# Output projection of a decoder layer: three pairs of row blocks multiplied by seven products each

## The chip, the cores and the metric

The kernel runs on one core of one Trainium2 chip. A core has a matrix engine (PE), a vector engine (DVE), a scalar engine (ACT), GpSimd (POOL) and a queue engine (SP) that only issues transfers. The time is the device time of one execution in microseconds; the time of the kernel before is the median of three runs. A profile of one execution gives the start and end of every instruction, counted from the first one.

## The reference

One decoder layer, 512 positions of width 1024, in float32. The change touches the output projection `mix`: the 2048 columns `[h, y]` (four mLSTM heads of 256 columns, then 1024 columns of a convolution group) times `w_out`, 2048 x 1024.

```python
u = rms_norm(x, mix_pre_g[l]) * (1.0 + sc1) + sh1
proj = u @ w_in[l]
...
h = mlstm_chunkwise(heads(q), heads(k), heads(v), ...)
h = rms_norm(h, ml_norm_g[l].reshape(H, Dh)).reshape(Bsz, S, D_ML)
h = h * jax.nn.sigmoid(o_pre)
...
y = causal_dwconv(a * jax.nn.sigmoid(gt), cv_dw_w[l], cv_dw_b[l])
y = jax.nn.silu(layer_norm(y, cv_ln_g[l], cv_ln_b[l]))

mix = jnp.concatenate([h, y], axis=-1) @ w_out[l]
x = x + g1 * rms_norm(mix, mix_post_g[l])

u = rms_norm(x, ffn_pre_g[l]) * (1.0 + sc2) + sh2
up = causal_dwconv(u @ ffn_up[l], ffn_conv_w[l], ffn_conv_b[l])
...
x = x + g2 * rms_norm(f, ffn_post_g[l])
```

## The kernel before

**Products.** Matrices are kept as a high part (rounded to the fast float32 format of PE) and a low part (the rest). `mm3` (lines 207 to 210) makes one product of a 128-row block by three matmuls: high by high, high by low, low by high. A weight piece, 128 x 512, is split by `w_split` (line 191: ACT copies the high part; line 192: POOL or DVE subtracts for the low part). `w_load` (line 199) loads up to four pieces at once into one of two `raws` buffers through SP's queue and splits them; the split pieces live in 20 `wpool` tiles, two a piece. Most other 128 x 512 tiles come from 36 `slots`; four `cvs` tiles (`cvtile`) serve as scratch. PSUM has four banks "mm", two "at" and two "cv".

**Order.** PE's and SP's instructions run in program order. The order on DVE, ACT and POOL is made at build time by a scheduler that simulates the engines and takes the ready instruction of highest priority, in general the one earliest in the program; `tc.cur_priority += LATER` puts what follows behind everything else. Each engine then executes its list in order. `behind(...)` and the manual dependence in `ada_block` force one instruction to stand after another on an engine.

**Heads.** `head_load` and `head_proj` make queries and keys, `make_vo` the values and the output gate (`vo`, one token tile of 128 positions after the other, eight row blocks each), `attention` (line 543) the scores (`s`, line 551), the outputs (`o`, line 562), the normalisation (lines 574 to 587) and the transposes (`hT`, line 593); lines 599 and 600 then split each of a head's two blocks of 128 columns into `hh` and `hl`. `attention` and `make_vo` are generators; `next(steps)` and `next(values)` lay their parts between the projections. The convolution taps run meanwhile on DVE, ACT and POOL; `norm_mean`, `norm_sums`, `norm_rows` and `norm_tiles` (lines 814 to 841) normalise their result into the eight blocks `yh`, `yl`. 

**Projection.** The sixteen row blocks of `w_out` are taken in the order `MIX`: heads 0 to 2 (blocks 0 to 5), y 8 to 13, head 3 (6 and 7), y 14 and 15. The left half of the 1024 output columns goes first (`mix_first`, into the four banks `mixa`, one for a token tile), between the steps of head 3's attention. The right half follows in the banks `mixb`: the first eight blocks in the loop at line 943, the other eight in `mix_last`, tile by tile, where each finished tile goes into the chain of norms (`chain_sums`, `chain_x`, `chain_u`) and on to the feed-forward part.

**Conditioning sums.** `ada_block` (line 176) loads half a megabyte through ACT's queue and multiplies it with the condition on DVE, summing each row. Sums 16 to 23 give the gains of `mixa`; sums 24 to 39 stand behind `last_lo`, head 3's last `hl`. They use two `ada` buffers and four parts of `spare`, which lies in the place of `u`'s low half once the last values are made. `ada_done` (line 181) and lines 948 to 950 make the gains of the feed-forward norm, `send_rows` (line 692) transposes them on PE (`gT`), stores them in DRAM and `row` loads them back as rows (`gs2r`, `sh2r`).

## Time and profile before

| | us |
|---|---|
| runs of the kernel | 767.45, 768.76, 769.22 (median 768.76) |
| span of the profiled execution | 767.4 |
| PE busy | 756.0 |
| DVE busy | 576.6 |
| POOL busy | 516.5 |
| ACT busy | 410.7 |
| mixa on PE, 192 matmuls of 128 x 512 | 317.2 to 368.5, with other pieces between |
| mixb up to `gT`, 96 matmuls | 368.5 to 390.3 |

The profile gives the execution's span, from its first to its last instruction; its time with what lies around the span isn't listed apart. A row of the timeline has the start, the duration, the engine, the line of the kernel, the operation, out<-in with their shapes, and in brackets how long the engine was idle before it and what released it. A row of the chain has start, duration, engine, what. PE's order on the chain is the program's, so the chain from 314 to 403 us shows the whole projection.

### The profile page before, as it was taken

The numbers are of one execution on the slowest core, as the hardware profiler recorded it, in microseconds if no ns is written. First come the engines' busy times: TensorE is split into PE (matmuls) and PEld (weight loads), VectorE is DVE, ScalarE is ACT, GpSimd is POOL, SyncE is SP. The second block draws the span as 40 slices with busy tenths as digits, with TensorE's granted clock in tenths as the row PEclk, the third lists the DMA queues.
The fourth block names the chain that finished last, engine by engine and source line by source line (L and its number), as shares of the span: only waits on it lengthen the run. The fifth ranks groups of instructions, "written<-read, shape, count | busy, mean of one in ns | idle before, by whom it ended". The sixth has DMA issues, their size and how long they took to land.

```text
span 767.4 us, 10129 instructions
## 1 busy us (share of the span) xinstructions
PE 756.0 (99%) x3480; PEld 625.1 (81%) x3480; DVE 576.6 (75%) x837; ACT 410.7 (54%) x778; POOL 516.5 (67%) x428
## 2 busy tenths in 40 slices
PE   7999999999999999999999999999999999999996
PEld 5778898878788788888889988888888888888885
DVE  6669999979979696476989978675684775654547
ACT  6675428585665655573345444443534444566633
POOL 4779849796494872645631179786887884599943
PEclk9999999999999999999999999999999999999999
DMA  8973313411131241655965755666767565796273
GB/s 317 349 281 113 112 56 117 158 56 56 55 111 56 98 168 64 235 199 168 365 222 183 271 210 191 240 219 247 262 231 275 187 239 185 271 397 241 93 249 135
DMA packets 40136, 147.32 MB, mean 192 GB/s; under 512 B 3826, under 2 KB 5266, under 8 KB 30484
## 3 DMA queue, kind: packets, MB, share of 16 engines
q1 hardware_dynamic: 27524, 96.59, 34.9%
q10 hardware_dynamic: 12560, 50.08, 18.3%
q8 instruction: 27, 0.44, 0.2%
q14 instruction: 25, 0.20, 0.1%
HBM read 126.59 MB, written 20.07 MB: 191 GB/s over the span
## 4 chain that ended last, share of the span: by engine, by line
PE 93%; DMA 4%; POOL 1%; ACT 1%; issue 0%; DVEq 0%; SPq 0%; DVE 0%; POOLq 0%; ACTq 0%
PE up L210 31%; PE dn L210 13%; PE qko L210 13%; PE vo L210 9%; PE glu L210 7%; PE mixa L210 6%; PE mixb L210 6%; DMA wglu<-in_w_glu 3%; PE o L562 2%; PE s L551 2%; PE v L210 2%; PE glu L350 1%; DMA xn<-in_x 1%; PE xT L992 0%; PE hT L593 0%
## 5 line engine op out<-in xcount | busy, mean ns | idle before, releaser
L774 DVE SCALAR_TENSOR_TENSOR cv<-gt,cvw,cv 128x485 f32<-128x485 f32 (+24 forms) x200 | 137.2, 731 | 2.1 <-ACT cv L762 0.8
L770 POOL TENSOR_TENSOR cs<-cs,cs 128x510 f32<-128x510 f32 (+3 forms) x32 | 42.1, 1316 | 0.2
L192 POOL TENSOR_TENSOR wup_0l<-wup,wup_0h 128x512 fp32r<-128x512 f32 x18 | 25.0, 1389 | 19.4 <-ACT wup_0h L191 19.3
L210 PE MATMUL up<-u2h,wup_0h 128*128 128x512 f32 (+1 forms) x96 | 35.8, 373 | 0.0
L210 PE MATMUL up<-u2h,wup_0l 128*128 128x512 f32 (+1 forms) x96 | 35.7, 371 | 0.0
L210 PE MATMUL up<-u2h,wup_512h 128*128 128x512 f32 (+1 forms) x96 | 35.6, 371 | 0.0
L210 PE MATMUL up<-u2l,wup_512h 128*128 128x512 f32 (+1 forms) x96 | 35.6, 371 | 0.0
L210 PE MATMUL up<-u2h,wup_512l 128*128 128x512 f32 (+1 forms) x96 | 35.6, 371 | 0.0
L210 PE MATMUL up<-u2l,wup_0h 128*128 128x512 f32 (+1 forms) x96 | 35.6, 371 | 0.0
L210 PE MATMUL up<-u2h,wup_1024h 128*128 128x512 f32 (+1 forms) x92 | 35.0, 381 | 0.0
L210 PE MATMUL up<-u2l,wup_1024h 128*128 128x512 f32 (+1 forms) x92 | 34.9, 380 | 0.0
L210 PE MATMUL up<-u2h,wup_1536l 128*128 128x512 f32 (+1 forms) x92 | 34.9, 380 | 0.0
L210 PE MATMUL up<-u2h,wup_1536h 128*128 128x512 f32 (+1 forms) x92 | 34.9, 380 | 0.0
L210 PE MATMUL up<-u2l,wup_1536h 128*128 128x512 f32 (+1 forms) x92 | 34.9, 380 | 0.0
L210 PE MATMUL up<-u2h,wup_1024l 128*128 128x512 f32 (+1 forms) x92 | 34.9, 380 | 0.0
L176 DVE SCALAR_TENSOR_TENSOR junk<-ada,cb 128x1024 bf16<-128x1024 f32 x20 | 29.9, 1493 | 2.6 <-DMA ada<-in_adaT 2.5
L768 ACT ACTIVATE cs<-gt,cvw 128x511 f32<-128x511 f32 (+4 forms) x40 | 27.1, 713 | 6.1 <-POOL cs L770 3.5
L192 POOL TENSOR_TENSOR wup_1536l<-wup,wup_1536h 128x512 fp32r<-128x512 f32 x18 | 24.6, 1365 | 6.0 <-ACT wup_1536h L191 5.4
L191 ACT ACTIVATE wup_512h<-wup 128x512 fp32r<-128x512 f32 x22 | 13.8, 629 | 25.7 <-PE up L210 20.9
L192 POOL TENSOR_TENSOR wup_1024l<-wup,wup_1024h 128x512 fp32r<-128x512 f32 x18 | 23.6, 1314 | 5.0 <-ACT wup_1024h L191 5.0
L330 DVE SCALAR_TENSOR_TENSOR junk<-ada,cps 128x1024 bf16<-128x1024 f32 x16 | 19.5, 1220 | 9.8 <-DMA ada<-in_adaT 9.2
L1113 DVE TENSOR_TENSOR b<-b 128x512 f32<-128x512 f32 x11 | 19.4, 1762 | 8.6 <-POOL b L1112 8.6
(1097 smaller groups left out, 2726.8 us busy)
## 6 DMA issues: line engine op xcount, KB each, us to landing
wup<-in_w_up SPq DMA_DIRECT2D x22, 1024.0 KB, 5.0
b<-in_w_down ACTq DMA_DIRECT2D x11, 1024.0 KB, 5.1
spill_t<-b ACTq DMA_DIRECT2D x11, 1024.0 KB, 3.9
ada<-in_adaT ACTq DMA_DIRECT2D x20, 512.0 KB, 4.8
wqko<-in_w_qko SPq DMA_DIRECT2D x9, 1024.0 KB, 4.8
ada<-in_adaT SPq DMA_DIRECT2D x16, 512.0 KB, 7.5
wo<-in_w_out SPq DMA_DIRECT2D x8, 1024.0 KB, 5.5
wvo<-in_w_vo SPq DMA_DIRECT2D x6, 1024.0 KB, 4.8
```

The lines of the kernel that those rows point to most:

```text
L176: t = V.scalar_tensor_tensor(out=junk, in0=r, scalar=1.0, in1=cb, op0=ALU.mult, op1=ALU.mult, accum_out=mod[:, i : i + 1])
L191: S.activation(hi[:, :n], src, AF.Copy)
L192: (eng or G).tensor_tensor(out=lo[:, :n], in0=src, in1=hi[:, :n].bitcast(F32), op=ALU.subtract)
L210: PE.matmul(ps, l, r, start=start and i == 0, stop=stop and i == 2, skip_group_check=again)
L330: V.scalar_tensor_tensor(out=junk, in0=first[k][:, i * D : (i + 1) * D], scalar=1.0, in1=cps, op0=ALU.mult, op1=ALU.mult, accum_out=part[: ...
L350: PE.matmul(ps, blk(wk, i)[a], u[k][b], start=k == 0 and p == 0, stop=k == KT - 1 and p == 1)
L551: PE.matmul(sp[:, :n], ks[d][:, cc * P : (cc + 1) * P], qs[d][:, cc * P :], start=d == 0, stop=d == 1)
L562: PE.matmul(o[:, : DH + 2], E[h][cc][:, a : a + P], vs[h][cc], start=cc == 0, stop=cc == tt)
L768: S.activation(t[:, d:], cvx[j][:, : T - d], AF.Copy, scale=w(CK - 1 - d))
L770: G.tensor_tensor(out=side[:, d:], in0=side[:, d:], in1=t[:, d:], op=ALU.add)
L774: tap = V.scalar_tensor_tensor(out=cp[:, d:], in0=cvx[j][:, : T - d], scalar=w(CK - 1 - d), in1=cp[:, d:], op0=ALU.mult, op1=ALU.add)
L1113: V.tensor_tensor(out=b22, in0=b22, in1=b11, op=ALU.subtract)
```

## The change

Each of heads 0 to 2 gives a pair of row blocks. With the 512 tokens cut into two halves of 256 (`HT`), the pair's two blocks of columns are a 2 x 2 matrix of left blocks, and the two row blocks of `w_out` with two halves of 512 columns are a 2 x 2 matrix of right blocks. The change makes the 2 x 2 result by seven block products (Winograd's form) and not eight: "11", "12", "22", "s1", "s2", "s3", "s4". "11", "12" and "s4" use blocks of `w_out` as they are; "s2", "s3", "22" and "s1" use sums of blocks. The sums of weights `mixq[1]` to `mixq[4]` are made in DRAM, by four copies on SP's queue and four adding transfers on POOL's. `left_parts` makes high and low parts and the sums of left blocks on ACT and POOL; `sums_split` splits the sums later. In `mixa` five products are made; the partial results K1, U2 and U3 are copied out of the banks into `cvs` tiles (`kept`) in between, and come in again by DVE, U2 and U3 in `mixb`, where "s1" and "s4" follow. A pair's weight loads are three pieces (`right_load`), of which every third piece's low part is made on DVE. The ten other blocks (`PLAIN`) stay as they were; in `mixb` two of them (`EARLY`) are laid between "s1" and "s4", and eight are left for `mix_last` as before. The values of head 3's last two token tiles are made together, block by block. Sums 24 to 27 of `ada_block` stand behind the last `yl` and no longer behind `last_lo`.

```diff
-MIX = [*range(6), *range(8, 14), 6, 7, 14, 15]
+PLAIN = [*range(8, 14), 6, 7, 14, 15]
+NP = len(PLAIN)
+PAIRS = 3
...
+        for tt in range(NT if h < H - 1 else 2):
+            ps = mmbank(f"vo{h}_{tt}")
+            some(tt, ps, range(KT))
+            values_out(tt, ps)
+            yield
+        if h == H - 1:
+            both = [mmbank(f"vo{h}_{tt}") for tt in (2, 3)]
+            for k in range(KT):
+                for tt, ps in zip((2, 3), both):
+                    some(tt, ps, [k])
+                if k == KT // 2 - 1:
+                    yield
+            for tt, ps in zip((2, 3), both):
+                values_out(tt, ps)
             yield
...
+    def left_parts(h, e, y):
+        z = left[h]
+        if e == 0:
+            halfy[h] = y
+            a11 = slot(f"ma{h}", F32R)
+            S.activation(a11[:, :HT], y[:, :HT], AF.Copy)
+            minus(a11[:, HT:], y[:, :HT], a11[:, :HT].bitcast(F32))
+            z["11"] = a11[:, :HT], a11[:, HT:], 0
+            return
+        x = halfy.pop(h)
+        hi, lo = slot(f"mh{h}", F32R), slot(f"ml{h}", F32R)
+        S.activation(hi, y, AF.Copy)
+        minus(lo, y, hi.bitcast(F32))
+        z["12"], z["22"] = (hi, lo, 0), (hi, lo, HT)
+        z["14"], z["23"] = a, b = slot(f"ms14_{h}"), slot(f"ms23_{h}")
+        minus(a[:, :HT], x[:, HT:], y[:, HT:])
+        minus(b[:, :HT], a[:, :HT], x[:, :HT])
+        minus(b[:, HT:], x[:, :HT], x[:, HT:])
+        G.tensor_tensor(out=a[:, HT:], in0=y[:, :HT], in1=b[:, :HT], op=ALU.add)
...
+    def mix_copies():
+        for q, a in ((1, 0), (3, 1), (2, 3), (4, 2)):
+            nc.sync.dma_start(mixq[q], w_mq[a])
+
+    def mix_add(q, src):
+        G.dma_start(mixq[q], src, accum_op=ALU.add, max_dma_last_dim=2048)
...
     head_load(0)
+    mix_copies()
...
+        if h < 2:
+            for q, src in ((1, w_mq[1]), (3, w_mq[3])) if h == 0 else ((2, mixq[1]), (4, mixq[2])):
+                mix_add(q, src)
...
+            out.append(w_split(r[:, p * T : (p + 1) * T], f"{name}_{p}", eng=V if V3[0] % 3 == 0 else G))
...
+    def mix_product(which, w, banks, p, start=False):
+        hi, lo, off = left[p][which]
+        for q, ps in enumerate(banks):
+            ts = slice(off + q * P, off + (q + 1) * P)
+            mm3(ps, (hi[:, ts], lo[:, ts]), w[p], start and p == 0, p == PAIRS - 1, True)
+
+    def kept(banks, name):
+        out = [cvtile(f"{name}{q}") for q in range(2)]
+        for t, ps in zip(out, banks):
+            S.activation(t, ps, AF.Copy)
+        return out
...
+    low, high = mixa[:2], mixa[2:]
+    s23 = upool.tile([P, KT, T], F32R, tag="uh", name="ms23")
+    w11 = right_load(w_mq[0], "m11")
+    sums_split("23", lambda p: (s23[:, 2 * p, :], s23[:, 2 * p + 1, :]), V)
     next(steps)
-    mix_first(0)
+    mix_product("11", w11, high, 0, True)
+    mix_product("11", w11, high, 1)
+    w21 = right_load(w_mq[2], "m21")
     next(steps)
...
+    mix_product("11", w11, high, 2)
+    k1 = kept(high, "mk1")
+    wt2 = right_load(mixq[2], "mt2")
+    mix_product("12", w21, low, 0, True)
     norm_rows()
     norm_tiles(0, 4)
...
+    for p in range(PAIRS):
+        mix_product("s2", wt2, high, p)
+    ku2 = kept(high, "mku2")
+    wt3 = right_load(mixq[3], "mt3")
+    mix_product("12", w21, low, 1)
+    for p in range(PAIRS):
+        mix_product("s3", wt3, high, p)
+    ku3 = kept(high, "mku3")
+    wt4 = right_load(mixq[4], "mt4")
+    mix_product("12", w21, low, 2)
+    for t, ps in zip(k1, low):
+        V.tensor_tensor(out=ps, in0=ps, in1=t, op=ALU.add)
+    sums_split("14", lambda p: (slot(f"ms14h{p}", F32R), slot(f"ms14l{p}", F32R)), G)
     next(steps)
     norm_tiles(4, KT)
...
+    for p in range(PAIRS):
+        mix_product("22", wt4, high, p)
     next(steps)
-    mix_first(6)
+    mix_first(0)
     next(steps)
-    for n in range(7, 10):
+    for n in range(1, 4):
         mix_first(n)
+    spare.append(upool.tile([P, KT, T], F32, tag="ul", name="spare"))
+    tc.cur_priority += LATER
+    for i in range(24, 28):
+        ada_block(i, last_yl[0])
+    tc.cur_priority -= LATER
     for _ in steps:
         pass
-    spare.append(upool.tile([P, KT, T], F32, tag="ul", name="spare"))
-    for i in range(24, 40):
+    for i in range(28, 40):
         ada_block(i, last_lo[0])
...
+    EARLY = 2
+    wt1 = right_load(mixq[1], "mt1")
+    wo = wo_rows(1, 0, EARLY)
+    for p in range(PAIRS):
+        mix_product("s1", wt1, banks[:2], p, True)
+    for t, ps in zip(ku3, banks):
+        V.tensor_tensor(out=t, in0=ps, in1=t, op=ALU.subtract)
+    for t, ps in zip(ku2, banks):
+        V.tensor_tensor(out=ps, in0=ps, in1=t, op=ALU.subtract)
+    w22 = right_load(w_mq[3], "m22")
+    for n in range(EARLY):
+        mix_plain(n, banks, wo[n], (2, 3), n == 0)
+    for p in range(PAIRS):
+        mix_product("s4", w22, banks[:2], p)
+    for t, ps in zip(ku3, banks[2:]):
+        V.tensor_tensor(out=ps, in0=ps, in1=t, op=ALU.add)
+    for n in range(EARLY):
+        mix_plain(n, banks, wo[n], (0, 1))
```

89 lines of the change are left out of this document (54 added, 35 removed).

## The prediction

> **What bounds the kernel now.** I read the page's first lines, then the chain of waits in order of time around the projection, then the busy time of each engine by stage, then VectorE's own timeline.
>
> ```profile
> span 767.4 us, 10129 instructions
> PE 756.0 (99%) x3480; PEld 625.1 (81%) x3480; DVE 576.6 (75%) x837; ACT 410.7 (54%) x778; POOL 516.5 (67%) x428
> ...
> PE 93%; DMA 4%; POOL 1%; ACT 1%; issue 0%; DVEq 0%; SPq 0%; DVE 0%; POOLq 0%; ACTq 0%
> ```
>
> PE is busy 99% of the span and holds 93% of the chain that ends last. The chain's rows (start, us, what) show where:
>
> ```profile
> 314.13 3.12 PE s L551 x8
> 317.24 2.73 PE mixa L210 x12
> ...
> 337.15 1.31 PE o L562 x6
> ...
> 342.95 8.21 PE mixa L210 x36
> 351.16 0.87 PE hT L593 x8
> ...
> 354.89 13.64 PE mixa L210 x60
> 368.53 21.76 PE mixb L210 x96
> 390.29 0.11 PE gT L692
> 390.40 12.97 PE mixb L210 x57
> ```
>
> From 314 to 403 us one PE piece follows another without a hole, so a matmul less there is worth its own time as long as everything else arrives as early as PE then wants it. Is there room for that? Busy time by stage (stretch, its us, then busy us of each engine):
>
> ```profile
> 157.00:258.00 101.00, 101.00 (x445) 82.07 (x445) 90.33 (x139) 64.77 (x143) 68.77 (x57) 1.00 0.18 63
> ...
> 314.00:343.00 29.00, 29.00 (x131) 23.44 (x131) 19.98 (x32) 18.67 (x40) 15.78 (x13) 1.00 0.70 251
> 343.00:353.70 10.70, 10.70 (x52) 8.90 (x51) 3.87 (x9) 5.68 (x13) 5.30 (x6) 1.00 0.22 89
> 353.70:388.60 34.90, 34.90 (x156) 28.79 (x155) 33.69 (x43) 10.74 (x23) 22.91 (x12) 1.00 0.90 317
> ```
>
> The last row matters most: between hT and gT, DVE is busy 33.69 of 34.90 us. It is nearly a second bound, hidden because PE has as much to do.
>
> **The removed matmuls.** 96 matmuls of mixb take 21.76 us, 0.2267 each. Before, the six row blocks of heads 0 to 2 cost 6 x 4 token tiles x 2 halves x 3 passes = 144. After, each pair costs 7 products x 2 tiles x 3 passes = 42, three pairs 126. That is 18 fewer, 18 x 0.2267 = **4.08 us**. It is not spread evenly: mixa grows from 192 to 210 matmuls (five products of 18, ten plain blocks of 12), so hT moves from 351.16 to 355.24 and the end of mixa from 368.53 to 372.61; the part of mixb ahead of gT shrinks from 96 to 60, so gT moves from 390.29 to 386.21. The reordered last values (tiles 2 and 3 together) are the same 48 matmuls: nothing on PE, and the weight buffers of their first half come free earlier.
>
> **DVE between hT and gT.** gT transposes the gains, which need all the ada sums; PE stands there until they are ready.
>
> ```profile
> 385.03 1.14 DVE L181 TENSOR_TENSOR mod<-mod,vec 128x16 f32<-128x16 f32 x1
> ...
> 387.44 1.24 DVE L950 TENSOR_SCALAR gains<-gains 128x8 f32<-128x8 f32 x1
> ```
>
> ```profile
> 353.70:388.60 34.90, 27.70 (x32) 1.00 0.90 317
> ```
>
> ```profile
> L940 DVE TENSOR_TENSOR mg<-mixa,g1r x4: 675/678/680, 371.3 to 374.2; 128x512 f32<-128x512 f32 x4
> ```
>
> The gains are ready at 388.7, 1.6 us ahead of gT. The middle row is line 176 alone in that stretch: 16 ada sums (two records each), 27.70 us, 1.73 each; the other DVE work there is 33.69 - 27.70 = 6.0. The change takes four of the 16 to an earlier place (after the last yl) and adds here four subtractions of kept values on PSUM (each like mg, 0.68: 2.7 us), every third weight split (two: 1.4) and two additions (1.4, wanted only after gT). The stretch itself shrinks: it starts 4.08 later and ends 4.08 earlier, from 353.7 to 390.29 now, 36.6 us, to 28.4. The need, with ada sums at 1.73: 12 x 1.73 + 6.0 + 4.1 = 30.9, that is 2.5 too much, 3.9 with the two additions in front. But an ada sum is 1.73 only in the mean:
>
> ```profile
> 353.68 1.22 DVE L176 SCALAR_TENSOR_TENSOR junk<-spare,cb 128x1024 bf16<-128x1024 f32 x1
> ...
> 382.80 2.19 DVE L176 SCALAR_TENSOR_TENSOR junk<-spare,cb 128x1024 bf16<-128x1024 f32 x1
> ```
>
> ```profile
> 315.66 1.28 POOL L192 TENSOR_TENSOR wo_1536l<-wo,wo_1536h 128x512 fp32r<-128x512 f32 x1
> ...
> 381.64 2.27 POOL L192 TENSOR_TENSOR wo_0l<-wo,wo_0h 128x512 fp32r<-128x512 f32 x1
> 383.87 2.27 POOL L192 TENSOR_TENSOR wo_512l<-wo,wo_512h 128x512 fp32r<-128x512 f32 x1
> ```
>
> Alone it takes 1.22 (1.30 with the read of its sum), beside a POOL subtraction 2.19, and that subtraction 2.27 instead of 1.28. At 1.30 the need is 12 x 1.30 + 6.0 + 4.1 = 25.7, less than 28.4. So the wait at gT lies between 0 and 3.9; with some ten POOL subtractions left in the stretch and two thirds of the collisions per sum I take 12 x 1.59 + 10.1 = 29.2, a wait of about **0.8 us**.
>
> Do the new subtractions collide with POOL too? They read one operand from PSUM and one from SBUF, as does E<-s:
>
> ```profile
> 315.99 0.69 DVE L552 SCALAR_TENSOR_TENSOR E<-s,E 128x512 f32<-128x512 f32 x1 [1.66 <-PE s L551]
> ```
>
> That one ran beside the POOL subtraction of 315.66 and took 0.69, so I keep 0.68. [...]
>
> **The new waits on kept values.** K1, U2 and U3 are copied out of the banks by ACT while PE waits to go on in them.
>
> ```profile
> L599 ACT ACTIVATE hh<-hT,ghalf x6: 674/686/702, 267.6 to 352.2; 128x512 fp32r<-128x512 f32 x6
> ```
>
> A copy out of PSUM is 0.69. Behind U2 stand six matmuls of product "12", 1.36 us, while the first bank's copy needs 0.69 and can begin 0.68 before the other bank is done: hidden unless ACT is busy for over half a microsecond. U3 is tighter: the six kept tiles share four buffers, so its copies wait until DVE has added K1 into the low banks. 0.68 (add) + 0.69 (copy) against 1.31 (the o matmuls in front of product "22") plus the 0.68 between the banks: 0.6 us of slack. An ada sum caught on DVE at 2.19 costs up to 1.6. In mixb, four subtractions (2.7 us) stand under twelve plain matmuls (2.72), and the second pair of products needs only the third of the four at its start; an ada sum in front costs 1.2 to 2.2 less the 0.7 of slack. If both happen, part of the DVE wait at gT is paid here instead, not twice. I take 0.5 for these beyond the 0.8 above; ends 0 and 3.
>
> **ACT and POOL before hT.** 41 weight pieces instead of 32 must be split.
>
> ```profile
> L191 ACT ACTIVATE wo_0h<-wo x8: 614/632/632, 284.8 to 377.6; 128x512 fp32r<-128x512 f32 x8
> L192 POOL TENSOR_TENSOR wo_0l<-wo,wo_0h x8: 1291/1362/2267, 287.4 to 381.6; 128x512 fp32r<-128x512 f32 x8
> ```
>
> In the stage 314 to 343, which becomes 33.1 us long, ACT gets six kept copies (4.1), six copies for the sums' halves (3.8) and about five more splits (3.2): 18.67 + 11.1 = 29.8, 90%. POOL gets about three splits (4.1) and the three "14" halves (4.1): 15.78 + 8.2 = 24. Both fit. What is late next if they don't is the first plain block's weights at 342.5, behind the eight norm tiles on ACT; twenty weight tiles hold ten pieces, over 13 us of PE work ahead, so I count nothing, with an end of 2. The four early ada sums fall where DVE is busy 3.87 of 10.70: 4 x 1.73 = 6.9 fits just, and hT has its own chain there:
>
> ```profile
> 347.79 1.71 ACT L585 ACTIVATE hn<-hn,fac 128x256 f32<-128x256 f32 x4 [1.58 <-DVE fac L581]
> ```
>
> hn is done at 349.5, hT at 351.16: 1.66 us of slack, and an ada sum in front of fac costs at most 2.19, so 0 to 0.5.
>
> **Parts of the left sums, copies and adding transfers.** Each head's left parts move two DVE operations to POOL, seven there of 256 or 512 columns, some 5 us at 1.3 per 512. POOL is idle 32 of the 101 us from 157 to 258, and nothing of it is wanted on PE before 317: free. Four DRAM copies go onto SP's queue behind the first head's loads, and four adding transfers onto POOL's queue.
>
> ```profile
> 101.23 32.06 SPq L199 DMA_DIRECT2D wqko<-in_w_qko  x4
> 141.74 7.81 SPq L199 DMA_DIRECT2D wvo<-in_w_vo  x2
> ```
>
> ```profile
> spill_t<-b ACTq DMA_DIRECT2D x11, 1024.0 KB, 3.9
> ...
> p<-spill_t SPq DMA_DIRECT2D x5, 1024.0 KB, 10.9
> ```
>
> The queue issues little there, the DMA share is 0.18 after 157, and the sums are first read after 300. An adding transfer isn't in this trace. By the nearest rows one of 768 KB lands in 3.9 to 10.9 us; POOL pays its issue only (I take nothing) or, at worst, stands for the whole landing. Below nothing there is no reason for a gain. [...]
>
> **Sum.** -4.08 + 0.8 (gT) + 0.5 (kept values) = -2.8. The profiled execution has a span of 767.4; the three runs are 767.45 to 769.22, so what lies around the span is small and I move the median by the same amount: 768.76 - 2.8 = **766.0**. All waits at zero: 764.7.
>
> **Rivals.**
> 1. DVE takes the gain back. Ada sums stay at 1.73 and the additions go first: wait 3.9, time 768.6. For it: 33.69 of 34.90 busy. Against: four sums leave, and POOL is less in their way. Without the additions in front, 2.5 and 767.2. I give 767.2 to 770.3 24%.
> 2. Slower: the kept values' subtractions queue behind all ada sums on DVE, which is in order. From 357.8, 12 x 1.73 + mg 2.7 + a split 0.7 end at 382.0, four subtractions at 384.7; the second products would start then and not at 379.41, 5.3 late, and with 30 matmuls after them gT comes at 391.5: 768.76 + 1.2 = 770.0, up to 771.5 with a wait at "22". It decides once over 4.08 is lost. For it: ada sums come first in the program. Against: mg, also later in the program, ran at 371.3 between two of them. 13%.
> 3. The adding transfers hold POOL: a landing of 10.9 in front of a weight's low half that PE waits for, with 5 us of lead left, gives about 772 less the gain, 770 to 772. For it: nothing in the trace. Against: POOL idles a third of that time, and ysq ended at 287.4 for a sum used at 300.68. 4%.
>
> ```profile
> 285.17 2.26 POOL L792 TENSOR_TENSOR ysq<-ysq,ydl 128x512 f32<-128x512 f32 x1
> ```
>
> ```profile
> 300.68 0.86 PE ytot L817 x2
> ```
>
> **How the numbers follow.** Forecast 766.0 with its own range 764.4 to 767.2: 59%. Within 0.2% (1.5 us, about what a measurement of this kernel can tell from no change): 24%, rival 1. Slower by more: 17%, rivals 2 and 3. Leaving out rival 2's upper part and rival 3, and a little below, 764.4 to 769.9 holds eight in ten.
>
> **What would show it.** Right: mixa 210 and mixb 156 matmuls; gT starts near 387 with the gains' last DVE operation just ahead; holes on PE of 1 to 2 us in sum between 317 and 390. Rival 1: a hole in front of gT released by the last DVE operation on the gains. Rival 2: a hole in front of the second products, released by a DVE subtraction that began long after the bank was ready. Rival 3: holes on PE between 157 and 300 behind POOL. It would all be wrong if PE's matmuls of the new order cost other than 0.2267, or if weights stand in front of PE.

## The result and the profile after

The changed kernel takes 801.26 us (median of four runs, 799.44 to 804.98) where the kernel before, beside it, takes 768.25. The ratio is 1.0436, with a 95% interval of 1.0406 to 1.0465: 33 us slower. The forecast was 766.0 with a range to 769.9, so it was wrong in sign and far outside its range.

The page of the changed kernel, in the lines that answer to those of before (span; busy time of each engine with its share and its instructions; the chain that ended last, by engine):

```profile
span 797.7 us, 10184 instructions
...
PE 765.3 (96%) x3462; PEld 627.4 (79%) x3462; DVE 602.4 (76%) x849; ACT 423.2 (53%) x805; POOL 542.0 (68%) x455
...
PE 73%; DVE 8%; issue 5%; POOL 4%; DMA 4%; ACT 4%; DVEq 0%; ACTq 0%; POOLq 0%; SPq 0%
```

PE has the 18 matmuls less that the change promised (3462 against 3480) and still is busy 9.3 us longer, and it holds 73% of the chain instead of 93%. So there are two losses: PE waits, and its matmuls take longer. What PE waited for (view of the waits; what waits, for what, us in all, times, longest):

```profile
PE Mb L701 <- DVE Mhl L732: 7.6, 1, 7.6
PE mixa L212 <- ACT mku L832: 4.2, 4, 3.3
PE mixb L212 <- DVE mixb L1073: 3.1, 1, 3.1
...
PE hT L648 <- ACT hn L640: 2.8, 1, 2.8
PE fcum L719 <- DVE g_lf L679: 1.7, 1, 1.7
PE s L606 <- DVE E L607: 1.6, 1, 1.6
PE o L617 <- ACT hn L621: 0.8, 1, 0.8
```

These seven rows sum to 21.8 us and none of them is in the same view of the kernel before. Two of them (`Mb`, the gate matrix of head 0, and `fcum`) lie 150 us ahead of the projection. The matmuls' part shows in the view of the cores (span, mean granted clock):

```profile
core 0: 797.7 us, clock 0.984
```

The clock before was 0.999. A loss of 1.6% of 797.7 us is 12.8 us, against 0.8 before. Where it goes is seen behind a wait, here the transposes of the last head and the products after them (timeline of PE):

```profile
380.49 2.53 PE L648 MATMUL hT<-ident,hn 128*128 128x128 f32 x8 [2.82 <-ACT hn L640]
...
384.10 0.63 PE L212 MATMUL mixa<-wo_0h,yh 128*128 128x512 f32 x1
384.53 0.63 PE L212 MATMUL mixa<-wo_0l,yh 128*128 128x512 f32 x1
...
387.59 0.39 PE L212 MATMUL mixa<-wo_512h,yh 128*128 128x512 f32 x1
387.82 0.40 PE L212 MATMUL mixa<-wo_512l,yh 128*128 128x512 f32 x1
```

After the wait of 2.82 us the products start 0.43 us apart, and from 387.1 us on 0.23 apart again. The view of stretches gives a granted clock of 0.50 from 380.3 to 387.1 us, so this wait costs 3.4 us beside itself. 21.8 of waits and 12.0 of clock, less the 4.1 that was saved, are 29.7; the span grew by 30.3.

The transposes of `u` after the projection (`xT<-ident,un`) show how far each part had fallen behind; in this view of a tile the times are those of the first and the last start. First before, then after:

```profile
L992 PE MATMUL xT<-ident,un x32: 270/272/273, 403.2 to 421.2; 128*128 128x128 f32 x32
```

```profile
L1126 PE MATMUL xT<-ident,un x32: 270/272/329, 432.8 to 451.4; 128*128 128x128 f32 x32
```

All 30.2 us are lost by the end of the projection. At the first product of `mixa` (first starts of that tile: 316.8 before, 330.3 after) it is 13.5; the other 16.7 are lost inside it.

**The first 13.5 us.** Timeline of GpSimd and of VectorE at the place:

```profile
125.22 1.18 POOL L596 DMA_DIRECT2D mixq<-in_w_mq  x1
126.13 1.61 POOL L194 TENSOR_TENSOR wqko_512l<-wqko,wqko_512h 128x512 fp32r<-128x512 f32 x1
127.39 1.56 POOL L194 TENSOR_TENSOR wqko_1024l<-wqko,wqko_1024h 128x512 fp32r<-128x512 f32 x1
138.88 0.97 POOL L596 DMA_DIRECT2D mixq<-in_w_mq  x1 [9.93 <-issue]
...
159.41 2.20 POOL L194 TENSOR_TENSOR wqko_1536l<-wqko,wqko_1536h 128x512 fp32r<-128x512 f32 x1
```

```profile
151.05 11.12 DVE L732 TENSOR_TENSOR Mhl<-Mr,Mhl 4x512 fp32r<-4x512 f32 x1
```

The scheduler put the four adding transfers at 125, 139, 147 and 158 us, right behind the copies and not in the idle time after 157. The second stood 9.93 us at the head of GpSimd's queue. The work behind it then ran without a gap from 138.9 to 161.6, and in that stretch VectorE's small subtraction for the gate matrix took 11.12 us. It ended about when GpSimd's stretch did, and `Mb` had waited for it. The same row of the kernel before, where GpSimd's stretch ended at 149.2:

```profile
145.84 3.90 DVE L671 TENSOR_TENSOR Mhl<-Mr,Mhl 4x512 fp32r<-4x512 f32 x1
```

The third and fourth transfer, 8.1 and 10.6 us behind the one ahead of them, did not stand.

### The profile page after: what moved, and what is told of

Same layout as the page of the kernel before. It is cut to its first block, busy times and chain, and to the rows that moved or that the text cites. A ratio compares the mean times of both kernels' runs of the same rounds, so it can differ in the third digit from the quotient of the medians.

```text
span 797.7 us, 10184 instructions
## 1 busy us (share of the span) xinstructions
PE 765.3 (96%) x3462; PEld 627.4 (79%) x3462; DVE 602.4 (76%) x849; ACT 423.2 (53%) x805; POOL 542.0 (68%) x455
## 4 chain that ended last, share of the span: by engine, by line
PE 73%; DVE 8%; issue 5%; POOL 4%; DMA 4%; ACT 4%; DVEq 0%; ACTq 0%; POOLq 0%; SPq 0%
PE up L212 29%; PE dn L212 10%; PE vo L212 8%; PE qko L212 8%; PE glu L212 7%; PE s L606 2%; PE mixa L212 2%; DMA wglu<-in_w_glu 2%; PE o L617 2%; PE v L212 1%; DVE Mhl L732 1%; DMA xr<-x1d 1%; DVE junk L178 1%; PE glu L352 1%; PE mixb L212 1%
## 5 line engine op out<-in xcount | busy, mean ns | idle before, releaser
L868 DVE SCALAR_TENSOR_TENSOR cv<-gt,cvw,cv 128x502 f32<-128x502 f32 (+21 forms) x200 | 136.8, 727 | 2.0 <-ACT cv L856 0.8
L864 POOL TENSOR_TENSOR cs<-cs,cs 128x510 f32<-128x510 f32 (+3 forms) x32 | 43.7, 1366 | 0.1
L194 POOL TENSOR_TENSOR wup_0l<-wup,wup_0h 128x512 fp32r<-128x512 f32 x18 | 26.3, 1459 | 17.5 <-ACT wup_0h L193 17.5
L1245 POOL TENSOR_TENSOR b<-b 128x512 f32<-128x512 f32 x11 | 14.7, 1333 | 16.9 <-DVE b L1244 13.2
L194 POOL TENSOR_TENSOR wup_1024l<-wup,wup_1024h 128x512 fp32r<-128x512 f32 x18 | 24.1, 1339 | 2.9 <-ACT wup_1024h L193 2.9
```

The lines of the kernel that those rows point to most:

```text
L194: (eng or G).tensor_tensor(out=lo[:, :n], in0=src, in1=hi[:, :n].bitcast(F32), op=ALU.subtract)
L864: G.tensor_tensor(out=side[:, d:], in0=side[:, d:], in1=t[:, d:], op=ALU.add)
L868: tap = V.scalar_tensor_tensor(out=cp[:, d:], in0=cvx[j][:, : T - d], scalar=w(CK - 1 - d), in1=cp[:, d:], op0=ALU.mult, op1=ALU.add)
L1245: G.tensor_tensor(out=b12, in0=b22, in1=b12, op=ALU.subtract)
```

## The experiments

"Over before" is the difference of the medians to the kernel before, run beside each on the same chip (767.70 to 769.02); gains between runs below are differences of that column.

| run | us | over before | ratio, 95% interval |
|---|---|---|---|
| the change | 801.26 | +33.0 | 1.0406 to 1.0465 |
| 1 change without sums of weights | 784.40 | +15.5 | 1.0174 to 1.0234 |
| 2 before with the transfers alone | 782.94 | +14.1 | 1.0156 to 1.0215 |
| 3 transfers held back | 790.47 | +21.6 | 1.0253 to 1.0313 |
| 4 and sums 24 to 27 in the old place | 786.26 | +17.4 | 1.0186 to 1.0270 |
| 5 run 2, other form of the subtraction | 782.26 | +13.8 | 1.0148 to 1.0207 |
| 6 change, other forms | 800.28 | +31.8 | 1.0382 to 1.0442 |
| 7 run 4, other forms | 791.86 | +23.4 | 1.0258 to 1.0346 |
| 8 run 7, other order of two queues | 792.60 | +24.1 | 1.0257 to 1.0367 |
| 9 run 2, one input from PSUM | 774.04 | +6.3 | 1.0049 to 1.0108 |
| 10 run 4, transfers spaced | 783.42 | +15.7 | 1.0171 to 1.0230 |
| 11 before with one transfer | 773.28 | +5.6 | 1.0048 to 1.0094 |
| 12 run 10, other order of two queues | 785.13 | +17.4 | 1.0174 to 1.0271 |
| 13 run 10 without the kept copies | 780.81 | +12.0 | 1.0107 to 1.0202 |
| 14 and without the left sums | 778.34 | +9.5 | 1.0085 to 1.0159 |
| 15 before with the paired last values | 768.81 | 0.0 | 0.9993 to 1.0012 |
| 16 run 10, gains turned later | 787.46 | +18.6 | 1.0196 to 1.0286 |
| 17 run 13, sums 24 to 27 early | 780.05 | +11.0 | 1.0120 to 1.0165 |
| 18 run 10, both moves on VectorE | 786.99 | +18.0 | 1.0205 to 1.0249 |

### Runs 1 and 2: the transfers, taken out and put in alone

```diff
-    mix_copies()
...
-        if h < 2:
-            for q, src in ((1, w_mq[1]), (3, w_mq[3])) if h == 0 else ((2, mixq[1]), (4, mixq[2])):
-                mix_add(q, src)
...
-    wt2 = right_load(mixq[2], "mt2")
+    wt2 = right_load(w_mq[3], "mt2")
```

> The changed kernel without the four copies and the four adding transfers; the sums of weights are left out, and the products that read them read plain weight tiles of the same size instead. Theory (the adding transfers stop GpSimd's queue between 125 and 158 us, the low parts of the weights behind them run late and without a gap, VectorE's subtraction for the gate matrix is locked out, and TensorE waits and loses its clock): 12 to 15 us less than the changed kernel, 786 to 789, the first scores of head 0 back at about 157.5 us of the span, the subtraction for the gate matrix at 4 us instead of 11. Rival (GpSimd is held by the new subtractions of the left parts, the transfers are free): 0 to 2 us less, about 799 to 801.

Run 2 adds to the kernel before the same four copies and the same loop of `mix_add`, nothing else.

> The kernel before with the four copies and the four adding transfers alone, at the places of the program where the change has them; nothing reads what they write. Theory (they hold GpSimd's queue): 11 to 13 us more than before, 779 to 781, with a hole on TensorE between 150 and 162 us of the span. Rival (the transfers are free beside the other traffic): within 1 us of before.

Run 1 is 17.5 under the change and run 2 14.1 over before; each is 1 to 2.5 us past its theory's range and far from the rival. Added up, 15.5 and 14.1 make 29.6 of the 33.0, so the two halves hardly depend on each other. In run 1 the subtraction for the gate matrix takes 1.38 us, and in run 2 PE waits for it as it does in the change:

```profile
PE Mb L651 <- DVE Mhl L682: 7.7, 1, 7.7
```

The copies and adding transfers are the cause of the first half: with nothing else of the change in the kernel, they cost 14 us. The four copies were not run alone, so their share isn't known.

### Runs 3 and 4: the transfers held back, and sums 24 to 27 in their old place

```diff
-        G.tensor_tensor(out=a[:, HT:], in0=y[:, :HT], in1=b[:, :HT], op=ALU.add)
+        end = G.tensor_tensor(out=a[:, HT:], in0=y[:, :HT], in1=b[:, :HT], op=ALU.add)
+        for q, src in {0: ((1, w_mq[1]), (3, w_mq[3])), 1: ((4, mixq[2]),)}.get(h, ()):
+            behind(mix_add(q, src), end)
...
-        if h < 2:
-            for q, src in ((1, w_mq[1]), (3, w_mq[3])) if h == 0 else ((2, mixq[1]), (4, mixq[2])):
-                mix_add(q, src)
...
-        G.tensor_tensor(out=fac, in0=ssq, in1=mhalf, op=ALU.pow)
+        end = G.tensor_tensor(out=fac, in0=ssq, in1=mhalf, op=ALU.pow)
+        if h == 1:
+            behind(mix_add(2, mixq[1]), end)
```

> The changed kernel with the same copies and adding transfers, but each of the four held back on GpSimd until its sources have long landed: two behind the last left part of head 0, one behind the norm factor of head 1, one behind the last left part of head 1. Theory (it is where they stand in GpSimd's queue that costs, not their traffic): 11 to 14 us less than the changed kernel, 787 to 790, close to the kernel without them. Rival (their traffic or their work costs wherever they stand): a few us less, 793 to 798, with the hole now between 190 and 280 us of the span.

```diff
-    for i in range(24, 28):
-        ada_block(i, last_yl[0])
...
-    for i in range(28, 40):
+    for i in range(24, 40):
         ada_block(i, last_lo[0])
```

> The previous kernel (adding transfers held back) with the modulation sums 24 to 27 again behind VectorE's last low part of the last head, where the kernel before has them, instead of ahead of it. Theory (those four sums stand on VectorE ahead of the last head's normalisation, and the 6.5 us wait of the last transposes is theirs): 3 to 6 us less than the kernel with the transfers held back, the wait for the last transposes under 1 us, part of it given back because the later sums delay the subtractions behind them. Rival (VectorE's work is only moved, the end of its queue sets the second products): within 1 us of that kernel.

Run 3 gained 11.4, at the low end of what was expected, but stays 6.1 over run 1 and so isn't close to the kernel without the transfers. Run 4 gained another 4.2, with PE's wait for the last transposes down from 1.9 to 0.5 us (in the change it was 2.8, not the 6.5 of the expectation). That part of the change, meant to relieve VectorE later, cost 4 us: the four sums stood ahead of the last head's normalisation on VectorE, and in the change ScalarE, whose queue issues their loads, stood 8.25 us for them too. What was left over at GpSimd is in its timeline of run 4, with VectorE's beside it:

```profile
231.18 1.07 POOL L598 DMA_DIRECT2D mixq<-in_w_mq  x1
240.78 0.97 POOL L598 DMA_DIRECT2D mixq<-in_w_mq  x1 [8.53 <-issue]
```

```profile
254.82 11.59 DVE L646 TENSOR_SCALAR hn<-hn,fac,rd 128x256 f32<-128x256 f32 x4
```

The copies had landed a hundred microseconds earlier, and the profile shows nothing that the second transfer still waited for. It stood 8.53 us all the same, and the backlog behind it locked out the normalisation of head 1. So the wait for a copy was not the cause; what stood, here and in the change, was a second adding transfer close behind the first (1.1 us here, 3.7 in the change).

### Runs 5, 6, 7 and 9: what locks VectorE out

The first guess was the form of the instruction, since the convolution taps, which are scalar_tensor_tensor, ran at 0.73 us in the same stretches.

```diff
-    V.tensor_tensor(out=Mhl[LO : LO + H, :], in0=Mr, in1=Mhl[:H, :].bitcast(F32), op=ALU.subtract)
+    V.scalar_tensor_tensor(out=Mhl[LO : LO + H, :], in0=Mr, scalar=1.0, in1=Mhl[:H, :].bitcast(F32), op0=ALU.mult, op1=ALU.subtract)
```

> The kernel before with the copies and adding transfers alone (as the second run had them), and one instruction of VectorE in another form: the subtraction that makes the low part of the gate matrix is a scalar_tensor_tensor with the scalar 1.0 instead of a tensor_tensor; the values are the same. Theory (a two-input tensor_tensor of VectorE on SBUF doesn't get in while GpSimd's instructions follow each other without a gap, a scalar_tensor_tensor does, as the taps and the modulation sums beside such stretches show): the subtraction takes about 1 us instead of 11.1, TensorE's wait of 7.7 us at the gate matrix falls below 2, and the kernel comes to 772 to 776 instead of 782.9. Rival (the subtraction is late because GpSimd's queue holds something that it needs, in whatever form it stands): 782 to 784, the wait stays.

In runs 6 and 7 the normalisation is changed in the same way, its second factor as a broadcast operand.

> The changed kernel, transfers at the places where the change has them, with two instructions of VectorE as scalar_tensor_tensor: the low part of the gate matrix, and the normalisation of heads 0 to 2 (with the second factor as a broadcast operand). Theory (lock-out of the two-input and two-scalar forms on SBUF): 7 to 10 us less than the changed kernel, 790 to 793. Rival (the low parts of the weights on GpSimd are late themselves and the wait only goes to the next product): 0 to 3 us less.

> The kernel with the adding transfers held back and the modulation sums 24 to 27 in their old place (786.3), with the same two instructions in the other form. Theory (the four normalisation instructions of head 1 took 11.6 us there beside a stretch of GpSimd without a gap, and the wait of 3.3 us at the transposes is theirs): 3 to 5 us less, 781 to 783, the normalisation at 0.5 to 0.8 us each. Rival (GpSimd's backlog is itself late): under 1 us less.

All three went against the theory: 782.26, 800.28 and 791.86. Runs 5 and 6 are where their rivals put them; run 7 is outside both, 6 us over run 4. Its four normalisations, now with a second input in SBUF, took 12.96 us, the wait at the transposes of head 1 grew from 3.3 to 4.9 us, and the clock fell from 0.993 to 0.985. The instruction in its new form, in run 5:

```profile
151.88 11.13 DVE L682 SCALAR_TENSOR_TENSOR Mhl<-Mr,Mhl 4x512 fp32r<-4x512 f32 x1
```

The taps read one input from PSUM. That was the next guess, and run 9 gives the subtraction such an input.

```diff
+    S.activation(aps[:H, :], Mr, AF.Copy)
-    V.tensor_tensor(out=Mhl[LO : LO + H, :], in0=Mr, in1=Mhl[:H, :].bitcast(F32), op=ALU.subtract)
+    V.tensor_tensor(out=Mhl[LO : LO + H, :], in0=aps[:H, :], in1=Mhl[:H, :].bitcast(F32), op=ALU.subtract)
```

> The kernel before with the copies and all four adding transfers (as in the second run), and the subtraction for the low part of the gate matrix reading one input from PSUM, where ScalarE copies it first; the values are the same. The form of the instruction didn't matter in the last runs, so the theory is now: an instruction of VectorE that takes both inputs from SBUF waits until GpSimd's instructions leave a gap, one with an input in PSUM doesn't (the convolution taps beside those stretches read PSUM). Theory: the subtraction takes 0.7 to 1.5 us instead of 11.1, the wait of 6 to 8 us at the gate matrix goes, 774 to 778. Rival (the low parts of the weights behind the waiting transfer are late themselves, so TensorE waits at the next product): the subtraction is short, the wait moves, 780 to 783.

It came to 774.04, 7.8 less than run 2, with no wait at the gate matrix, while GpSimd's second transfer stood 9.86 us as before:

```profile
151.05 0.68 DVE L683 TENSOR_TENSOR Mhl<-aT,Mhl 4x512 fp32r<-4x512 f32 x1
```

So 11.1 us against 0.68, at the same moment and beside the same stretch of GpSimd, and the only difference is where one input lies (and ScalarE's copy that puts it there). Of the 6.3 us that are left in run 9, 2.8 are waits of PE (`fcum`, `s`, `o`) and about 3 are clock (0.995). A lock-out doesn't take two tiles in SBUF: the normalisation of run 4 reads one, with a column of factors for each of its two scalars, and took 11.59 us for four. In the change VectorE's 11.12 us, from 151.05 to 162.17, lie beside the last eight instructions of GpSimd's stretch, which ended at 161.6.

How long VectorE waits beside such a stretch differs, though. In the kernel before, the gate matrix's subtraction also waited until the stretch ended. But the four normalisations of head 0 there took 5.24 us beside GpSimd instructions from 203.1 to 209.5 us without a gap, one such instruction's time each, and in run 10 those of head 1 get in the same way beside a stretch from 255.0 to 266.4:

```profile
256.76 4.65 DVE L646 TENSOR_SCALAR hn<-hn,fac,rd 128x256 f32<-128x256 f32 x4
```

What decides between the two isn't shown. The waits of VectorE of over 10 us (11.12 in the change, 11.13 in run 5, 11.59 in run 4, 12.96 in run 7) stand beside a stretch with an adding transfer in it or right ahead of it.

### Runs 10 and 11: how far apart the transfers must stand, and what one costs

Run 10 is run 4 with the first transfer moved behind the norm factor of head 0, some 33 us ahead of the second.

> The kernel with the adding transfers held back and the modulation sums 24 to 27 in their old place (786.3), with the first adding transfer moved ahead by itself, behind the norm factor of head 0, so that no two adding transfers follow each other within 20 us. Theory (the second of two neighbours stands until the first has landed, 8.5 us in that kernel although the program gives it no wait, and GpSimd's backlog behind it locks out the normalisation of head 1): GpSimd has no idle stretch ahead of a transfer, the normalisation takes under 1 us an instruction, the wait of 3.3 us at the transposes goes, 780 to 783. Rival (the transfers hold GpSimd whatever their distance): 785 to 787.

> The kernel before with the four copies and the first adding transfer alone. Theory (the cost of the four, 14 us, comes from transfers that stand in GpSimd's queue until an earlier one has landed; one alone stands for nothing): within 1.5 us of before, 768 to 770. Rival (each transfer and its traffic costs its share): 3 to 4 us over before, 771.5 to 773.

Run 10 gave 783.42, 1.7 less than run 4 and just past its range; no transfer stood, and the normalisation took at most 1.4 us an instruction (under 1 was expected). Run 11 missed both numbers: +5.6 for one transfer, more than its rival's 3 to 4. Its transfer stands for nothing, but at 125 us GpSimd has no gap around it and VectorE is locked out again, now in a subtraction 16 columns wide that the forget gates need:

```profile
126.10 4.33 DVE L629 SCALAR_TENSOR_TENSOR g_lf<-gz,g_fl 128x16 f32<-128x16 f32 x1
```

Before, the same instruction took 0.70 beside GpSimd instructions that follow each other without a gap:

```profile
126.41 0.70 DVE L619 SCALAR_TENSOR_TENSOR g_lf<-gz,g_fl 128x16 f32<-128x16 f32 x1
```

PE waits 2.8 us for it in run 11 and the clock is 0.995 (0.999 before). So the place costs too, not only the neighbour.

Run 10 has the whole change and the cheapest places for the transfers. Its first product of `mixa` starts at 317.3, 0.5 later than before, and its last transposes of `u` at 435.6, 14.4 later, so what stays lost lies in the projection alone:

```profile
PE mixb L212 <- DVE mixb L1070: 3.7, 2, 3.6
PE mixa L212 <- ACT mku L836: 3.0, 4, 1.9
...
PE s L608 <- DVE E L609: 1.6, 1, 1.6
...
PE gT L757 <- DVE gains L1082: 0.6, 1, 0.6
PE hT L652 <- ACT hn L644: 0.4, 1, 0.4
```

The waits are 9.3 us. Part of the rest is clock: busy time by stretches of 4 us around two of them (stretch, its us, busy us of PE, PEld, DVE, ACT and POOL, granted clock, DMA share, GB/s):

```profile
320.00:324.00 4.00, 2.38 (x12) 1.51 (x10) 4.00 (x5) 0.90 (x2) 3.83 (x3) 0.94 1.00 342
324.00:328.00 4.00, 4.00 (x14) 3.20 (x13) 3.28 (x7) 1.20 (x2) 0.00 (x0) 0.64 0.73 238
...
392.00:396.00 4.00, 1.64 (x5) 1.09 (x6) 4.00 (x7) 2.50 (x7) 3.30 (x3) 0.90 1.03 403
396.00:400.00 4.00, 4.00 (x14) 3.17 (x13) 3.96 (x7) 1.26 (x2) 1.57 (x2) 0.68 1.08 398
```

After waits of 1.6 and 3.6 us the clock is 0.64 and 0.68 for a stretch; in finer stretches it is 0.50 for 3.4 us. Counted from start to start in PE's timeline, some 30 single matmuls of the products took 0.3 to 0.6 us each, about 6 us beyond 0.2267 apiece. With the waits, less the 4.1 saved, that is 11.2 of the 14.4 us; some 3 us are not accounted for.

What a wait costs in clock can't be read from its length alone. The same wait of 1.6 us at `s` was followed by a clock of 1.00 in the change (335 to 343 us) and in run 13 (320 to 328), and so was one of 3.3 us at head 1's transposes in run 4 (270 to 274). Waits of 3.6 us in run 10 and 4.7 in run 14 were followed by half rate for 3.4 us, waits of 5.4 in run 14, 5.7 in run 13 and 7.6 in the change for 6.7 or 6.8. Shorter ones had it too: in the change 1.7 (`fcum`), 3.1 (`mixb`) and 3.3 us (`mixa`) were followed by half rate for 3.4 us, and 2.8 (`hT`) for 6.8.

### Runs 8, 12, 16 and 18: other orders of the same work

Each moves instructions of VectorE, ScalarE or PE in run 7 or run 10 so that a wait shown there should go. The core of the diffs:

```diff
# runs 8, 12, 16, 18: behind the subtractions on the second products' banks
+    for tt, ps in enumerate(mixa):
+        behind(V.tensor_tensor(out=mg[tt], in0=ps, in1=g1r[0], op=ALU.mult), last_sub)
# run 8: the activations of norm tiles 2 to 7 behind the kept copies, sums 34 to 39 behind last_sub
# run 12: the kept copies of the second product on VectorE
# run 16: send_rows(KT, 2 * KT) behind mix_last(0, 0, LAST)
# run 18: sums 24 to 27 right behind 20 to 23
```

> The previous kernel with two queues put in another order: ScalarE copies the kept values of the second product ahead of the activations of the norm's tiles 2 to 7, and VectorE makes the subtractions on the second products' banks ahead of the last six modulation sums and of the products with the gain row. Theory (the waits of 3.3 us in the first products and of 3.6 us in the second products stand behind those queues, each with a lower clock after it): 6 to 9 us less than the previous kernel, 773 to 777, both waits under 1 us. Rival (the work is only moved: the wait goes to the transposes of the gains, which need VectorE's last sums): 2 to 4 us less, with a wait of 3 to 5 us at the gains' transposes.

> The kernel with the spaced transfers, with the kept values of the second product copied by VectorE instead of ScalarE, and the products with the gain row put behind the subtractions on the second products' banks on VectorE. Theory (each wait of TensorE over 2 us costs itself and about as much again in the lower clock after it): the wait for the kept values falls from 3 to 1 us, that of the second products from 3.6 to 1.3, together 5 to 7 us less than the kernel with the spaced transfers. Rival (the transposes of the gains take the time back, as in the last call's fourth kernel): 0 to 2 us less, with a wait of 3 us or more at the gains' transposes.

> The kernel with the spaced transfers; on VectorE the products with the gain row stand behind the subtractions on the second products' banks, and on TensorE the transposes of the gains behind the first tile's last products. Theory (each wait costs itself and the lower clock after it, and the gains' transposes took the gain back only because they stood ahead of products that could have run): the wait of 3.7 us at the second products falls to about 1.5 and none appears at the gains, 3 to 5 us less, 778 to 781. Rival (the time is taken back later, as the rows that the transposes make come later for the first tile's chain): within 1.5 us of 783.4.

> The kernel with the spaced transfers and its computation complete (783.4), with both moves on VectorE: sums 24 to 27 right behind 20 to 23, and the products with the gain row behind the subtractions on the second products' banks. Theory (the second products wait less, and the gains no longer come late for it): 4 to 8 us less, 775 to 779, still over the kernel before, as the waits for the kept copies (3.0 us) and for the last head's scores (1.6 us) stay. Rival (each move only passes the wait on): 781 or more.

None gained: 792.60, 785.13, 787.46 and 786.99 (the two times of run 16 lie 5.6 us apart). The wait at the second products fell to 1.4 us or less in runs 8, 12 and 16 and stayed at 3.8 in run 18; that for the kept copies fell in none. And each has a new or longer one: 8.8 and 4.7 us at the gains' transposes in runs 8 and 12, 3.9 us at the transposes of `u` in run 16, 8.1 us for the kept copies in run 18.

### Runs 13, 14, 15 and 17: the side work taken out

```diff
# run 13, against run 10
-    k1 = kept(high, "mk1")
...
-    ku2 = kept(high, "mku2")
...
-    for t, ps in zip(ku2, banks):
-        V.tensor_tensor(out=ps, in0=ps, in1=t, op=ALU.subtract)
# run 14, against run 13
-    sums_split("23", lambda p: (s23[:, 2 * p, :], s23[:, 2 * p + 1, :]), V)
...
-        mix_product("s2", wt2, high, p)
+        mix_product("12", wt2, high, p)
```

> The kernel with the spaced transfers (783.4), without the copies of kept products, their additions and their subtractions; the products run on in their banks, so the combination of the seven products is left out. Theory (the waits of 3.0 us for the copies and 3.7 us for the subtractions, with some 5 us of half-speed matmuls behind them, are the larger part of what stays lost): 9 to 12 us less, 771 to 775, with no wait over 1 us at the first and second products. Rival (VectorE and ScalarE set the end of the stage through the modulation sums in any case): 2 to 4 us less, with a wait at the gains' transposes.

> The previous kernel, in which also the sums and differences of the left parts and their splits are left out; the four products that read them read the split halves instead. What stays is the same number of matmuls and the same loads and splits of weights. Theory (the 18 matmuls saved are worth their 4.1 us as soon as nothing waits): 2 to 6 us less than the previous kernel, the wait of 1.6 us in the last head's scores gone, 765 to 770; at 763 to 765 the saving would be whole. Rival (the products by halves run slower than the plain ones for a reason of their own, their weights coming from other queues): 771 or more, with slow matmuls where no wait stands ahead of them.

> The kernel before with the last head's values of tiles 2 and 3 made as a pair, block of weights by block, and nothing else of the change. Theory (a change of order among products whose operands are all there): within 0.2% of before. Rival (the two tiles come out together at the end and the last head waits for them): 1 to 3 us more.

> The kernel without the kept copies, their additions and subtractions (the combination of the seven products is left out, as there), with the modulation sums 24 to 27 on VectorE right behind sums 20 to 23, ahead of the last head's chain instead of behind it. Theory (the wait of 5.7 us at the gains' transposes is the length of VectorE's queue of sixteen sums, which the kernel before hides behind 96 early products and this one only behind 60): the wait falls to 1 us or less, and with the lower clock after it 5 to 8 us go, 771 to 774. Rival (the sums ahead of the chain delay the last head as in the change): the wait moves to the last head's transposes, within 2 us.

Run 15 is as expected: the paired last values change nothing. Run 13 gave 780.81 (two runs, 777.86 and 783.76), on its rival's side. Run 14 gave 778.34 (776.14 and 780.53): the 2.5 us that it gains on run 13 are less than its own two runs differ by, and the time is far over the 765 to 770 of its theory. The slow matmuls of its rival, with no wait ahead of them, aren't there either: the clock is 1.00 from 305 to 360 us, 0.50 for 3.4 us behind the wait at `hT`, 1.00 again and 0.50 for 6.7 us behind the wait at `gT`. So even the products without the kept copies and without the left sums, with 18 matmuls fewer, are 9.5 us slower than before. In run 13 the waits at the products are gone and one stands where the rival put it:

```profile
PE gT L757 <- DVE gains L1071: 5.7, 1, 5.7
```

Its reason is in three rows of run 13's timelines, the transposes of the last head and VectorE's first and last work on the way to the gains:

```profile
358.71 1.96 PE L652 MATMUL hT<-ident,hn 128*128 128x128 f32 x8 [0.68 <-ACT hn L644]
```

```profile
363.54 1.21 DVE L178 SCALAR_TENSOR_TENSOR junk<-spare,cb 128x1024 bf16<-128x1024 f32 x1
...
396.19 0.17 DVE L1071 TENSOR_SCALAR gains<-gains 128x8 f32<-128x8 f32 x1
```

From the first of the sixteen sums behind the last head to the gains VectorE needs 32.8 us here, some 2 of them standing for the sums' loads; before it was 35.0. No matmul saved makes this shorter, and it cannot begin before `hT`, which comes at 358.7 instead of 351.0, 4.1 us of that because `mixa` has 18 matmuls more and the rest by waits. From `hT` to the first sum it is 4.8 us instead of 2.7. Before, 96 early matmuls of `mixb` covered that queue; now 60 do.

One thing in these traces was not tried. ScalarE too executes its list in order, and the split of the right half's first weights, `mt`, stands in it ahead of the last head's normalisation. In run 14 ScalarE stands there 5.33 us, up to 354.07, for a load that SP issued at 349.75. Head 3's last sum of squares is next in its list, VectorE waits 3.47 us for that sum, and PE waits at `hT`:

```profile
PE gT L752 <- DVE gains L1063: 5.4, 1, 5.4
PE hT L647 <- ACT hn L639: 4.7, 1, 4.7
```

The two waits shown and about 5.4 us of clock, less the 4.1 saved, make the 11.4 us by which run 14's profiled execution is longer than before. How much of it an earlier load or a later split of `mt` would give back was not tested; in run 13 ScalarE stands 6.78 us at the same place, but what it makes next waits as long for VectorE.

Run 17 then puts four of the sums ahead of the last head, and the wait is at that head's own chain:

```profile
PE hT L652 <- ACT hn L644: 4.5, 1, 4.5
...
PE o L619 <- ACT hn L623: 2.3, 1, 2.3
```

At 780.05 it is within run 13's spread. The theory fell and the rival held: the wait changes its place. The last head's chain from its last `o` to `hT` was 8.0 us before (343.0 to 351.0), under 36 matmuls on PE; in run 17 it is 12.7 (352.3 to 364.9), on engines that have more to do.

## Why the prediction was wrong

**"Free", the copies and adding transfers.** This is the step that failed first. It took nothing for them, on the idle time of GpSimd from 157 to 258, and named as the worst that GpSimd stands for a whole landing of 3.9 to 10.9 us. Run 2 measured 14.1 us. The standing was within those ends (9.93 and 8.53 us), but two things were missed. The transfers' place was taken from the need (read after 300) instead of from the program, where they stand right behind the loads of heads 1 and 2, and the scheduler puts what is ready there. And the price of standing was taken to be the lateness of weights, when it was VectorE, locked out by the backlog. Rival 3 had the cause, "the adding transfers hold POOL", with holes on PE between 157 and 300; it was given 4% and 770 to 772, with a weight's low half as the thing that is late.

**4.08 us for 18 matmuls.** The count is right: the trace has 210 and 156. Their worth isn't: PE was not the only bound of the stage. The prediction had read that VectorE is busy 33.69 of 34.90 us between `hT` and `gT` and weighed it as a wait of 0.8 us, 3.9 at most. Run 13, with all sixteen sums behind the last head as before, shows 5.7 us there. In the changed kernel itself this wait doesn't appear, since PE is late for other reasons.

**0.5 us for the kept values, ends 0 and 3.** Measured: 4.2 us in `mixa` and 3.1 in `mixb`. The copies waited behind activations on ScalarE, the subtractions behind the sums and the gain row's products on VectorE, which is rival 2's mechanism, given 13%. ScalarE at 90% of a stretch was called a fit; in an engine that runs its list in order, such a share says little about when one short copy gets its turn.

**Nothing for ScalarE and GpSimd before `hT`, and 0 to 0.5 for `hT` itself.** Measured 1.6 (`s`), 0.8 (`o`) and 2.8 us (`hT`); run 4 shows that the moved sums 24 to 27 alone cost 4.2. The 1.6 is VectorE's, which the prediction gave no new work in this stage: from 330.2 to 337.3 us it makes three low parts of the left sums and two of weights, 6.4 us, between the instructions on `E` that PE waits for.

**A term that wasn't there.** The prediction said it would be wrong if PE's matmuls cost other than 0.2267. They cost 0.43 for 3.4 or 6.8 us behind five of the seven waits, 12.0 us lost in all. The 6.8 us stand behind the waits of 7.6 (`Mb`) and 2.8 us (`hT`). In run 10 a wait of 1.6 us was followed by half rate for 3.4 us, in run 13 the same wait by none, so what sets it off isn't shown.

**The rivals** were counted as alternatives, and they came together. Rival 3 was priced at 1 to 3 us over before and cost 14.1; rival 2's wait, priced at 5.3, was 3.1; rival 1's, priced at 3.9, was 5.7 in run 13 and hidden in the change.

What stays open: why a second adding transfer stands, when VectorE is locked out for a whole stretch and when for one GpSimd instruction, some 3 us of run 10, and how much of run 14's 9.5 us the late `mt` costs; that the rest is VectorE's queue of sums is read from the rows, and no run took that queue away. No run was faster than the kernel before; the cheapest with the whole computation is run 10.

## What to carry to other kernels

A stage in which a second engine is busy 97% of the time gave nothing for fewer matmuls, and moving that engine's work ahead only helps where no chain of the next step stands in the way. An engine that runs its list in order and stands for a late load can hold up the chain that comes next in its list (in run 14 ScalarE stood 5.33 us for `mt`, and PE then waited 4.7 us at `hT`). A transfer that GpSimd issues is an instruction of GpSimd's queue: look up where the scheduler will put it, keep a second one away from the first (1 and 3.7 us behind it stood, 8.1 us behind it didn't), and ask which VectorE instructions that read SBUF alone fall beside the backlog; an input in PSUM took the one that was tried out of it (0.68 us for 11.1). The half rate behind a wait of PE of 3.6 to 7.6 us cost 1.7 to 3.4 us more in the runs above, half of the 3.4 to 6.8 us that it lasted; behind one of 1.6 us it cost 1.7 in run 10 and nothing in run 13.

## What the runs showed of the hardware

- A two-input VectorE subtraction of 4 x 512 on SBUF took 11.1 us beside a stretch of GpSimd without a gap, as tensor_tensor (the change) and as scalar_tensor_tensor (run 5), and 0.68 with one input in PSUM (run 9); in the kernel before, beside a shorter stretch, it took 3.90. A normalisation of four instructions on SBUF took 11.6 us beside such a stretch in run 4, and 4.65 and 5.24 beside others in run 10 and in the kernel before.
- A second adding transfer (768 KB, DRAM to DRAM) 1 us behind the first stood 8.53 us in run 4 with nothing shown that it waited for, and one 3.7 us behind stood 9.93 us in the change. The two that followed there after 8.1 and 10.6 us did not stand.
- In the change 768 KB copied within DRAM landed after 10.8 us in the median, the adding transfers after 10.3 and 7.5.
- PE's granted clock fell to 0.50 for 3.4 us (0.64 over 4 us) after a wait of 1.6 us in run 10, and stayed at 1.00 after the same wait in run 13 and after one of 3.3 us in run 4.
